# A two-layer decoder trunk: part of layer 1's down projection as seven block products

## The chip, the cores and the metric

The kernel runs on one core of a Trainium2 chip. The metric is the device time in microseconds of one execution; for each kernel the median of several runs is given.

## The reference

Input `x` is 1 x 512 x 1024 in float32. Two layers follow one another, each a mixer and a gated FFN with a convolution, both with a pre-RMSNorm and a residual, and a final RMSNorm. The part that matters here is the FFN (`D_FF` = 2816):

```python
def gated_conv_ffn(x, w_gate, w_up, conv_w, conv_b, w_down):
    g = jnp.einsum('bsd,df->bsf', x, w_gate)
    g = causal_dwconv3(g, conv_w) + conv_b
    up = jnp.einsum('bsd,df->bsf', x, w_up)
    return jnp.einsum('bsf,fd->bsd', jax.nn.silu(g) * up, w_down)
...
        hn = rms_norm(h, norm_ffn[layer])
        h = h + gated_conv_ffn(hn, w_ffn_gate[layer], w_ffn_up[layer], ...)
    return rms_norm(h, final_norm)
```

## The kernel before

The 2816 hidden channels are 22 tiles of 128 (`ft` = 0 to 21), the 512 tokens four tiles, the 1024 output columns two halves of 512. Every float32 factor is split in a high part (rounded to the fast float32r form, by ScalarE) and a low part (the rest, by VectorE), and each product is three matmuls: high x high, high x low, low x high (`mm3`, lines 132 to 135). `parts` (line 125) splits a weight tile of 128 x 1024 so. `summed` (line 116) does it without VectorE: ScalarE writes the negated high part, a DMA from GpSimd's queue adds the raw tile to it, and ScalarE writes the high part.

Hidden tiles are made in pairs `f`, `f` + 1. Pairs 0 and 2 are computed directly (`direct`). Pairs 4, 6, 10, 14, 18 go through `both`: the gate and the up projection are each cut into 2 x 2 blocks and computed with seven block products in place of eight (Strassen's way, in Winograd's form), from sums of weight blocks (`s12`, `s34`) and sums of activation blocks that stand ready (`t23`, `t41`). Pairs 8, 12, 16, 20 go through `seven`, which does so for the up projection alone; the gate is done directly (`gates(0)`, `gates(1)`). A `seven` or `both` product is 12 matmuls of 256 columns.

In layer 1 (`ffn1`) the down projection is done in groups, `PARTS`: after pairs 0 and 2 for tiles 0 and 1, after pair 4 for tiles 2 to 5, and from then on after every `both` and `seven` for four tiles. `act` (line 516) splits each activation tile into `a_hi` and `a_lo` as soon as it is there. `group8` (line 1035) multiplies: the stationary operand is an activation tile of 128 tokens, the moving one a weight row block of 512 columns; eight outputs (four token tiles, two halves) have a PSUM bank each, and when an output's last matmul is done VectorE adds the bank to `y` (line 1010). The last group also does the final norm and stores.

The order on each engine is not the program's. A scheduler takes what is ready by its own estimate, in order of place in the program, and gives out buffers in the same way; `inorder` (`keep_in_program_order`) pins an instruction behind the one traced before it on its engine. What limits how far it reaches ahead are the rings of buffers: `raw` 4 (weights as loaded), `whi` and `wlo` 6 each (split weights), `sum` 3 (sums of weights), `ahi` and `alo` 4 each (split activations), `s` 3, and seven PSUM banks.

Of the kernel before, what the change touches and what calls it, by code (L numbers as in the profile page):

```python
# [15 lines left out]
P = 128  # L16
# [14 lines left out]
def tile_trunk(ctx: ExitStack, tc: tile.TileContext, x, norm_mix, norm_ffn, final_norm,  # L31
# [99 lines left out]

    def mm3(ps, lhs, rhs, start, stop):
        nc.tensor.matmul(ps, lhs[0], rhs[0], start=start, stop=False)  # L133
        nc.tensor.matmul(ps, lhs[0], rhs[1], start=False, stop=False)  # L134
        nc.tensor.matmul(ps, lhs[1], rhs[0], start=False, stop=stop)  # L135
# [352 lines left out]
    class Ffn:  # L488
# [7 lines left out]

        def __init__(self, layer, prm, norm, ap, sums):
            self.layer, self.prm, self.ap, self.acts = layer, prm, ap, {}
            self.norm, self.sums = norm, sums
            self.t23, self.t41 = {}, {}  # L500

        def conv(self, t, ft):
            ap, prm, n = self.ap, self.prm, f"{self.layer}_{ft}"
            c = ap.tile([P, S], F32, tag="c", bufs=2, name=f"c{n}")
            nc.scalar.activation(c, t[:, 0:S], AF.Copy, scale=prm("cf", ft))
            for i in (1, 2):
                nc.vector.scalar_tensor_tensor(c, t[:, i : S + i], prm("cf", i * NF + ft), c,  # L507
                                               op0=ALU.mult, op1=ALU.add)
            return c

        def silu(self, c, ft):
            s = self.ap.tile([P, S], F32, tag="s", bufs=3, name=f"s{self.layer}_{ft}")
            nc.scalar.activation(s, c, AF.Silu, bias=self.prm("bf", ft))  # L513
            return s

        def act(self, ft, s):
            self.acts[ft] = split(self.ap, s, f"a{self.layer}_{ft}", tag="a", bufs=4)

# [190 lines left out]

        def seven(self, f):  # L710
            layer, ap, n = self.layer, self.ap, f"{self.layer}_{f}"
# [56 lines left out]
            def add(i, ps):  # L768
                nc.vector.tensor_tensor(kept[:, i, :], ps, kept[:, i, :], ALU.add)

            keep(0, multiply(1))
# [21 lines left out]
            nc.vector.tensor_tensor(s0, kept[:, :2, :], s0, ALU.mult)  # L793
            self.act(f, s[0])

        def hidden(self, f, before=lambda i, j: None):
            if f == 0:
                def first(i, j):
                    before(i, j)
                    if (i, j) == (1, 0):  # L800
                        self.norm.rstd_tokens()
                    elif (i, j) == (2, 2):
                        self.r = self.norm.rstd_spread()

                ch = self.pair_weights(0, [("g", 0), ("u", 0), ("g", 1), ("u", 1)])
                rest = self.direct(0, False, (range(4),), ch, first)
                self.ch = self.pair_weights(2, [("g", 0), ("g", 1), ("u", 0), ("u", 1)], "g")
                for kp in range(NP):
                    self.normalize(kp)
                rest()  # L810
            elif f == 2:
                self.direct(2, True, ((0, 1), (2, 3)), self.ch)()
            elif f % 4 == 2 or f == 4:
                self.both(f)
            else:
                self.seven(f)

# [142 lines left out]
    def ffn1(norm):  # L960
        with tc.tile_pool(name="f1", bufs=1) as ap:
# [3 lines left out]

            ffn = Ffn(1, prm1, norm, ap, sums)
            acts = ffn.acts
            y = [ap.tile([P, D], F32, name=f"y{t}") for t in range(NT)]
            ssf = ap.tile([P, NT, PAD], F32, name="ssf")[:, :, :2]
# [11 lines left out]

            for groups, a, b in PARTS:
# [24 lines left out]
                def done(j, ps):  # L1007
# [7 lines left out]
                    nc.scalar.activation(sq, dst, AF.Square, accum_out=ss)  # L1015
                    yf[half] = ap.tile([P, S], F32, tag="s", bufs=3, name=f"yf{j}")
                    nc.vector.tensor_tensor(yf[half], dst, fin[:, half * 512 : (half + 1) * 512],
# [17 lines left out]
    def group8(name, ks, lhs, rhs, tail, on_done):  # L1035
# [45 lines left out]
```

## Time and profile before

| | |
|---|---|
| median of 3 runs | 1005.43 us (1005.26 to 1005.86) |
| span of the profiled execution, first to last instruction | 1004.4 us |
| median less span | 1.0 us |
| TensorE busy | 992.1 us |
| VectorE busy | 666.0 us |
| ScalarE busy | 499.9 us |
| GpSimd busy | 94.1 us |
| mean granted TensorE clock | 0.999 |

Busy times are of the one profiled execution. PE is TensorE's matmuls, PEld its weight loads, DVE is VectorE, ACT ScalarE, POOL GpSimd, SP the queue that issues most loads. `u_8a` is the bank of product "a" of the up projection of pair 8, `dn` a bank of the down projection. A matmul's printed duration is its latency; start-to-start distances tell what one costs. In brackets behind a row stands the idle time ahead of it and what ended it.

### The profile page before, as it was taken

The numbers are of one execution on the slowest core, as the hardware profiler recorded it, in microseconds if no ns is written. First come the engines' busy times: TensorE is split into PE (matmuls) and PEld (weight loads), VectorE is DVE, ScalarE is ACT, GpSimd is POOL, SyncE is SP. The second block draws the span as 40 slices with busy tenths as digits, with TensorE's granted clock in tenths as the row PEclk, the third lists the DMA queues.
The fourth block names the chain that finished last, engine by engine and source line by source line (L and its number), as shares of the span: only waits on it lengthen the run. The fifth ranks groups of instructions, "written<-read, shape, count | busy, mean of one in ns | idle before, by whom it ended". The sixth has DMA issues, their size and how long they took to land.

```text
span 1004.4 us, 14019 instructions
## 1 busy us (share of the span) xinstructions
PE 992.1 (99%) x5547; PEld 865.9 (86%) x5547; DVE 666.0 (66%) x993; ACT 499.9 (50%) x735; POOL 94.1 (9%) x109
## 2 busy tenths in 40 slices
PE   8999999999999999999999999999999999999997
PEld 6888888898989989899878888888989898898985
DVE  5977457968584775847833645389675857658567
ACT  6523345754553635537645434675535365353553
POOL 3032030200000000000300001212000000000000
PEclk9999999999999999999999999999999999999999
DMA  7532234554445444454433123435545345353432
GB/s 236 178 105 84 85 90 122 117 155 114 118 142 131 128 110 119 138 137 127 127 125 104 63 85 105 101 88 123 150 100 153 105 127 147 94 152 112 127 85 84
DMA packets 80749, 120.30 MB, mean 120 GB/s; under 512 B 4164, under 2 KB 53548, under 8 KB 80684
## 3 DMA queue, kind: packets, MB, share of 16 engines
q1 hardware_dynamic: 73580, 98.96, 30.9%
q0 software_dynamic: 5760, 18.88, 10.7%
q10 hardware_dynamic: 1344, 1.58, 0.5%
q8 instruction: 43, 0.70, 0.3%
q14 instruction: 22, 0.18, 0.1%
HBM read 98.42 MB, written 2.10 MB: 100 GB/s over the span
## 4 chain that ended last, share of the span: by engine, by line
PE 95%; DMA 2%; DVE 2%; ACT 1%; SPq 0%; issue 0%; POOL 0%; DVEq 0%; ACTq 0%; POOLq 0%
PE dn L133 4%; PE dn L135 4%; PE dn L134 4%; PE d L133 4%; PE d L134 4%; PE d L135 4%; PE gu L133 3%; PE g L133 3%; PE g L134 3%; PE gu L134 3%; PE gu L135 3%; PE g L135 3%; PE u L135 1%; PE oo L133 1%; PE oo L135 1%; PE u L134 1%
## 5 line engine op out<-in xcount | busy, mean ns | idle before, releaser
L507 DVE SCALAR_TENSOR_TENSOR c<-rows,prm,c 128x512 f32<-128x512 f32 x88 | 68.9, 792 | 0.3
L134 PE MATMUL d<-a_lo,whi_d 128*128 128x512 f32 x176 | 68.6, 390 | 0.0
L135 PE MATMUL d<-a_hi,wlo_d 128*128 128x512 f32 x176 | 68.5, 389 | 0.0
L133 PE MATMUL dn<-whi_dn,a_hi 128*128 128x512 f32 x176 | 68.4, 390 | 0.0
L134 PE MATMUL dn<-wlo_dn,a_hi 128*128 128x512 f32 x176 | 68.4, 390 | 0.0
L135 PE MATMUL dn<-whi_dn,a_lo 128*128 128x512 f32 x176 | 67.6, 390 | 0.0
L133 PE MATMUL d<-a_hi,whi_d 128*128 128x512 f32 x176 | 67.1, 390 | 0.0
L1010 DVE TENSOR_TENSOR y<-dn,y 128x512 f32<-128x512 f32 x48 | 32.3, 688 | 30.9 <-PE dn L135 30.7
L133 PE MATMUL g<-hgh,whi_g 128*128 128x512 f32 x128 | 50.0, 391 | 0.0
L134 PE MATMUL g<-hgl,whi_g 128*128 128x512 f32 x128 | 50.0, 391 | 0.0
L135 PE MATMUL g<-hgh,wlo_g 128*128 128x512 f32 x128 | 49.8, 389 | 0.0
L129 DVE TENSOR_TENSOR wlo_dn<-raw_dn,whi_dn 128x1024 fp32r<-128x1024 f32 x22 | 26.8, 1222 | 30.7 <-ACT whi_dn L128 30.7
L129 DVE TENSOR_TENSOR wlo_d<-raw_d,whi_d 128x1024 fp32r<-128x1024 f32 x22 | 26.8, 1221 | 30.2 <-ACT whi_d L128 30.2
L129 DVE TENSOR_TENSOR wlo_u<-raw_u,whi_u 128x1024 fp32r<-128x1024 f32 x16 | 19.6, 1223 | 34.2 <-ACT whi_u L128 34.1
L120 ACT ACTIVATE wlo_g<-raw_g 128x1024 fp32r<-128x1024 f32 x14 | 14.7, 1050 | 51.6 <-PE dn L134 51.6
L292 DVE TENSOR_TENSOR h<-d,h 128x512 f32<-128x512 f32 x48 | 32.4, 686 | 11.6 <-PE d L135 11.1
L513 ACT ACTIVATE s<-c,prm 128x512 f32<-128x512 f32 x44 | 31.6, 718 | 16.7 <-DVE c L507 16.6
L135 PEld LDWEIGHTS dn<-whi_dn,a_lo 128*128 128x128 f32 x176 | 33.0, 188 | 7.4 <-DVE a_lo L249 0.2
L134 PEld LDWEIGHTS d<-a_lo,whi_d 128*128 128x128 f32 x176 | 33.1, 188 | 7.1 <-DVE a_lo L249 0.2
L133 PEld LDWEIGHTS dn<-whi_dn,a_hi 128*128 128x128 f32 x176 | 33.1, 188 | 7.0 <-ACT a_hi L247 0.2
L133 PEld LDWEIGHTS d<-a_hi,whi_d 128*128 128x128 f32 x176 | 32.9, 188 | 7.0
L135 PEld LDWEIGHTS d<-a_hi,wlo_d 128*128 128x128 f32 x176 | 33.0, 188 | 6.8
(972 smaller groups left out, 3196.0 us busy)
## 6 DMA issues: line engine op xcount, KB each, us to landing
raw_g<-in_w_ffn_gate_dram SPq DMA_DIRECT2D x36, 512.0 KB, 4.5
raw_u<-in_w_ffn_up_dram SPq DMA_DIRECT2D x36, 512.0 KB, 3.8
raw_d<-in_w_ffn_down_dram SPq DMA_DIRECT2D x22, 512.0 KB, 3.6
raw_dn<-in_w_ffn_down_dram SPq DMA_DIRECT2D x22, 512.0 KB, 4.4
wlo_u<-raw_u POOLq DMA_DIRECT2D x18, 512.0 KB, 5.2
wlo_g<-raw_g POOLq DMA_DIRECT2D x14, 512.0 KB, 4.5
raw_oe<-in_w_out_even_dram SPq DMA_DIRECT2D x8, 512.0 KB, 3.5
raw_g<-in_w_ffn_gate_dram SPq DMA_DIRECT2D x16, 256.0 KB, 2.9
```

What stands on the lines that cost most here:

```text
L120: nc.scalar.activation(lo, raw, AF.Copy, scale=-1.0)
L129: nc.vector.tensor_tensor(lo, raw, hi.bitcast(F32), ALU.subtract)
L133: nc.tensor.matmul(ps, lhs[0], rhs[0], start=start, stop=False)
L134: nc.tensor.matmul(ps, lhs[0], rhs[1], start=False, stop=False)
L135: nc.tensor.matmul(ps, lhs[1], rhs[0], start=False, stop=stop)
L292: nc.vector.tensor_tensor(h[k], ps, h[k], ALU.add)
L507: nc.vector.scalar_tensor_tensor(c, t[:, i : S + i], prm("cf", i * NF + ft), c, op0=ALU.mult, op1=ALU.add)
L513: nc.scalar.activation(s, c, AF.Silu, bias=self.prm("bf", ft))
L1010: nc.vector.tensor_tensor(dst, ps, dst, ALU.add)
```

## The change

Tiles 2 to 17 of layer 1's down projection leave `group8`. Four tiles `a` to `a` + 3 are taken as a 2 x 2 block product: two pairs of hidden tiles, two halves of the tokens, two halves of the columns. `down(a)` computes it with seven block products of 12 matmuls (128 x 512) instead of 96 matmuls in one go. It is a generator: each `yield` ends a step, and `seven` calls `step()` at eight places between its own products, so the down products of tiles 2 to 5 lie within pair 8, those of 6 to 9 within pair 12, 10 to 13 within 16, 14 to 17 within 20. Each product accumulates in a bank (`a`, `b` or `e`, one per token tile), and after each product VectorE adds its two banks to `y`. The sums of weights are t1 (in place, in the first raw tile) and t2, t3, t4 in tiles of their own (ring `sum`). The activations are kept unsplit, in pairs (ring `s`, now four tiles of 128 x 2 x 512), and split when a product needs them (`part`, ring `ahi`/`alo`, now three). The down projection of tiles 0 and 1 now follows pair 4 instead of pair 2. Tile 20 is split into a `sum` tile. `c` moves to another pool, `y` becomes one tile, and `group8` pins the first matmul of each three.

```diff
-    def mm3(ps, lhs, rhs, start, stop):
-        nc.tensor.matmul(ps, lhs[0], rhs[0], start=start, stop=False)
+    def mm3(ps, lhs, rhs, start, stop, order=lambda ins: ins):
+        order(nc.tensor.matmul(ps, lhs[0], rhs[0], start=start, stop=False))
...
-            c = ap.tile([P, S], F32, tag="c", bufs=2, name=f"c{n}")
+            c = tp.tile([P, S], F32, tag="sq", name=f"c{n}")
...
         def silu(self, c, ft):
-            s = self.ap.tile([P, S], F32, tag="s", bufs=3, name=f"s{self.layer}_{ft}")
+            f = ft - ft % 2
+            if f not in self.rows:
+                self.rows[f] = self.ap.tile([P, 2, S], F32, tag="s",
+                                            bufs=4 if self.layer else 3,
+                                            name=f"s{self.layer}_{f}")
+            s = self.rows[f][:, ft % 2, :]
             nc.scalar.activation(s, c, AF.Silu, bias=self.prm("bf", ft))
             return s
 
         def act(self, ft, s):
-            self.acts[ft] = split(self.ap, s, f"a{self.layer}_{ft}", tag="a", bufs=4)
+            if ft == NF - 2 and self.kept:
+                both = self.ap.tile([P, 2, S], F32R, tag="sum", bufs=3, name="a_last")
...
+            elif ft not in self.kept:
+                self.acts[ft] = split(self.ap, s, f"a{self.layer}_{ft}", tag="a",
+                                      bufs=4 if self.layer == 0 else 3)
...
             keep(0, multiply(1))
+            step()
             gates(0)
+            step()
             keep(1, multiply(6))
             gates(1)
+            step()
             c, s = [], []
             for j in range(2):
                 t = padded_tile()
                 nc.scalar.copy(t[:, 2:], banks[j])
                 c.append(self.conv(t, f + j))
+            step()
             keep(2, multiply(7))
             for j in range(2):
                 s.append(self.silu(c[j], f + j))
+            step()
             ps = multiply(5)
+            step()
             p2 = multiply(2)
             add(2, ps)
             add(0, p2)
+            step()
             ps = multiply(4)
...
             self.act(f, s[0])
+            step()
...
+            def part(a, src, n):
+                hi = ap.tile([P, 2, HALF], F32R, tag="ahi", bufs=3, name=f"hi{n}_{a}")
+                lo = ap.tile([P, 2, HALF], F32R, tag="alo", bufs=3, name=f"lo{n}_{a}")
+                nc.scalar.activation(hi, src, AF.Copy)
+                nc.vector.tensor_tensor(lo, src, hi.bitcast(F32), ALU.subtract)
+                return hi, lo
+
+            def down(a):
...
+                g1, g2 = ffn.rows[a], ffn.rows[a + 2]
+                a11, a21 = g1[:, :, :HALF], g1[:, :, HALF:]
+                a12, a22 = g2[:, :, :HALF], g2[:, :, HALF:]
...
+                def multiply(product, at, half, c):
+                    (hi, lo), (whi, wlo) = stat[product], mov[product]
+                    for i in range(2):
+                        first = (at, i) not in banks
+                        if first:
+                            banks[at, i] = mm_bank(f"{name}{at}{i}")
+                        ps = banks[at, i]
+                        ts_ = slice(i * P, (i + 1) * P)
+                        for k in range(2):
+                            for l, r, end in ((hi, whi, False), (hi, wlo, False),
+                                              (lo, whi, k == 1)):
+                                nc.tensor.matmul(ps, l[:, k, ts_], r[:, k, :], start=first,
+                                                 stop=end, skip_group_check=True)
+                                first = False
+                        dst = y[2 * half + i][:, c * 512 : (c + 1) * 512]
+                        nc.vector.tensor_tensor(dst, ps, dst, ALU.add)
...
+                b11, b12, b22, b21 = block(0, 0), block(0, 1), block(1, 1), block(1, 0)
+                mov[1] = parts(*b11)
+                stat[1] = part(a, a11, 1)
+                t1 = b11[0]
+                minus(t1, b12[0], b11[0])
...
+                nc.vector.tensor_tensor(s1, a21, a22, ALU.add)
+                minus(s2, s1, a11)
+                yield
+                multiply(1, "a", 0, 0)
+                stat[2] = part(a, a12, 2)
+                mov[2] = parts(*b21)
+                t2 = t_tile(2)
+                minus(t2, b22[0], t1)
+                yield
+                multiply(2, "b", 0, 0)
+                stat[6] = part(a, s2, 6)
+                mov[6] = parts(t2, 2, 512, f"{name}_t2")
+                yield
+                multiply(6, "a", 0, 1)
+                stat[5] = part(a, s1, 5)
+                mov[5] = parts(t1, 2, 512, f"{name}_t1")
+                t3 = t_tile(3)
+                minus(t3, b22[0], b12[0])
+                minus(s1, a11, a21)
+                yield
+                multiply(5, "e", 1, 1)
+                stat[7] = part(a, s1, 7)
+                mov[7] = summed(t3, 2, 512, f"{name}_t3")
+                minus(s2, a12, s2)
+                yield
+                multiply(7, "a", 1, 1)
+                stat[3] = part(a, s2, 3)
+                mov[3] = parts(*b22)
+                t4 = t_tile(4)
+                minus(t4, b21[0], t2)
+                yield
+                multiply(3, "e", 0, 1)
+                stat[4] = part(a, a22, 4)
+                mov[4] = summed(t4, 2, 512, f"{name}_t4")
+                yield
+                multiply(4, "a", 1, 0)
+                yield
+
+            for groups, a, b in (((0, 2, 4), 0, 2), ((6, 8), 2, 6), ((10, 12), 6, 10),
+                                 ((14, 16), 10, 14), ((18, 20), 14, 18), ((), 18, 22)):
                 for f in groups:
-                    ffn.hidden(f, before=before)
+                    steps = down(a) if f > 6 and f % 4 == 0 else None
+                    ffn.hidden(f, before=before, steps=steps)
                 last = b == NF
+                if a in (2, 6, 10, 14):
+                    continue
...
-            mm3(banks[j], lhs(ks[i], j), rhs(ks[i], j), i == 0, i == len(ks) - 1)
+            mm3(banks[j], lhs(ks[i], j), rhs(ks[i], j), i == 0, i == len(ks) - 1, inorder)
```

More of the change, by code (lines that the diff above doesn't have):

```diff
@@ L488, in tile_trunk, with __init__ @@
     class Ffn:
-        def __init__(self, layer, prm, norm, ap, sums):
+        def __init__(self, layer, prm, norm, ap, sums, kept=()):
             self.layer, self.prm, self.ap, self.acts = layer, prm, ap, {}
@@ L708, in both, with seven @@
             self.act(f, s[0])
-        def seven(self, f):
+        def seven(self, f, steps=None):
             layer, ap, n = self.layer, self.ap, f"{self.layer}_{f}"
@@ L769, in add, with step @@
                 nc.vector.tensor_tensor(kept[:, i, :], ps, kept[:, i, :], ALU.add)
+            def step():
+                if steps is not None:
+                    next(steps)
             keep(0, multiply(1))
+            step()
             gates(0)
+            step()
             keep(1, multiply(6))
             gates(1)
+            step()
             c, s = [], []
@@ L794, in seven, with hidden @@
             self.act(f, s[0])
-        def hidden(self, f, before=lambda i, j: None):
+            step()
+        def hidden(self, f, before=lambda i, j: None, steps=None):
             if f == 0:
@@ L815, in hidden @@
             else:
-                self.seven(f)
+                self.seven(f, steps)
     def ffn0(norm):
@@ L964, in sums @@
                         for k in (kp, kp + NP)]
-            ffn = Ffn(1, prm1, norm, ap, sums)
+            ffn = Ffn(1, prm1, norm, ap, sums, range(2, 18))
             acts = ffn.acts
-            y = [ap.tile([P, D], F32, name=f"y{t}") for t in range(NT)]
+            y_all = ap.tile([P, NT, D], F32, name="y")
+            y = [y_all[:, t, :] for t in range(NT)]
             ssf = ap.tile([P, NT, PAD], F32, name="ssf")[:, :, :2]
@@ L980, in before, with minus @@
                     turn_residual(j, i)
-            for groups, a, b in PARTS:
+            def minus(dst, x, y_):
+                nc.vector.tensor_tensor(dst, x, y_, ALU.subtract)
+            def part(a, src, n):
[4 more added lines that the diff above has]
+                return hi, lo
@@ L1015, in done @@
                     nc.scalar.activation(sq, dst, AF.Square, accum_out=ss)
-                    yf[half] = ap.tile([P, S], F32, tag="s", bufs=3, name=f"yf{j}")
+                    if half == 0:
+                        yf["pair"] = ap.tile([P, 2, S], F32, tag="s", bufs=4, name=f"yf{j}")
+                    yf[half] = yf["pair"][:, half, :]
                     nc.vector.tensor_tensor(yf[half], dst, fin[:, half * 512 : (half + 1) * 512],
```

19 lines of the change are left out of this document (17 added, 2 removed).

## The prediction

> **What bounds the kernel now.** I read the page first (busy shares, then the chain that ended last), then the windows of one period of layer 1's FFN, then the PE, VectorE and ScalarE timelines inside it, and last the waits.
>
> ```profile
> span 1004.4 us, 14019 instructions
> PE 992.1 (99%) x5547; PEld 865.9 (86%) x5547; DVE 666.0 (66%) x993; ACT 499.9 (50%) x735; POOL 94.1 (9%) x109
> ...
> PE 95%; DMA 2%; DVE 2%; ACT 1%; SPq 0%; issue 0%; POOL 0%; DVEq 0%; ACTq 0%; POOLq 0%
> ```
>
> TensorE is busy 99% of the span and holds 95% of the chain: time goes only by taking matmuls away or by making them wait. The profiled span is 1004.4 us and the median of the runs is 1005.43, so 1.0 us lies outside the span; I work out the change of the span and add it to the median. Layer 1's FFN repeats a period: a pair of hidden tiles by `both`, a pair by `seven`, then the down projection of four tiles. The windows of one period, in that order (columns: us, PE, PEld, DVE, ACT, POOL busy with counts, clock, DMA share, GB/s), and then the whole period:
>
> ```profile
> 745.80:764.70 18.90, 18.90 (x159) 18.79 (x158) 12.08 (x18) 10.95 (x18) 0.86 (x1) 1.00 0.57 157
> 764.70:785.70 21.00, 21.00 (x134) 19.09 (x133) 14.52 (x22) 13.86 (x22) 0.85 (x1) 1.00 0.55 151
> 785.70:809.00 23.30, 23.30 (x111) 19.48 (x110) 15.53 (x25) 6.03 (x7) 0.86 (x1) 1.00 0.28 77
> ```
> ```profile
> 745.80:809.00 63.20, 63.20 (x399) 57.35 (x398) 42.13 (x63) 30.85 (x46) 2.57 (x3) 1.00 0.46 125
> ```
>
> TensorE has no gap, at full clock. VectorE has 21 us of 63.2 to spare, ScalarE 32.
>
> **What goes.** The first matmul of this period's down projection, and the first behind it:
>
> ```profile
> 785.55 0.40 PE L133 MATMUL dn<-whi_dn,a_hi 128*128 128x512 f32 x1
> ...
> 807.36 0.28 PE L624 MATMUL g_10a<-hgh,whi_a 128*128 128x256 f32 x1
> ```
>
> In between are 4 tiles x 8 outputs x 3 = 96 matmuls in 21.81 us: 0.227 us each (the 0.40 printed is latency; they are pipelined). Seven products of 2 x 2 x 3 = 12 matmuls of the same shape make 84, so a group saves 12 x 0.227 = 2.73 us. Four groups are changed (tiles 2-5, 6-9, 10-13, 14-17): 10.9 us. A kernel that stays dense on TensorE would take 1005.4 - 10.9 = 994.5 us; that is the floor.
>
> **What comes on VectorE.** The groups of the next period, and four rows of the VectorE timeline for the true spacing:
>
> ```profile
> L1010 DVE TENSOR_TENSOR y<-dn,y 128x512 f32<-128x512 f32 x8 | 5.4, 690 | 7.7 <-PE dn L135 7.7
> L129 DVE TENSOR_TENSOR wlo_dn<-raw_dn,whi_dn 128x1024 fp32r<-128x1024 f32 x4 | 4.9, 1221 | 6.4 <-ACT whi_dn L128 6.4
> L249 DVE TENSOR_TENSOR a_lo<-s,a_hi 128x512 fp32r<-128x512 f32 x4 | 2.7, 684 | 0.0
> ```
> ```profile
> 746.30 1.22 DVE L634 TENSOR_TENSOR wlo_s12u<-s12u,whi_s12u 128x1024 fp32r<-128x1024 f32 x1
> 747.43 0.69 DVE L730 TENSOR_TENSOR s<-raw_u,raw_u 128x512 f32<-128x512 f32 x1
> 748.03 0.69 DVE L732 TENSOR_TENSOR s<-raw_u 128x512 f32<-128x512 f32 x1
> 748.64 0.69 DVE L731 TENSOR_TENSOR s<-s,raw_u 128x512 f32<-128x512 f32 x1
> ```
>
> Back to back, a 1024-wide instruction takes 1.13 us from start to start and a 512-wide one 0.605. Before, a group has 4 wide (`wlo_dn`) and 12 narrow (4 `a_lo`, 8 additions to `y`): 4 x 1.13 + 12 x 0.605 = 11.8 us. After, it has 9 wide (t1 to t4, five `parts`) and 25 narrow (four sums of activations, seven low parts, 14 additions): 10.2 + 15.1 = 25.3 us. That is 13.5 us more. The period becomes 63.2 - 2.7 = 60.5 us for TensorE and 42.1 + 13.5 = 55.6 us for VectorE, 92% of it. The stretch in which the products lie, `seven` and down together, is 21.0 + 23.3 - 2.7 = 41.6 us for TensorE, and holds 14.5 + 15.5 + 13.5 = 43.5 us for VectorE: 1.9 us too much, which must go into `both`'s stretch, where 18.9 - 12.1 = 6.8 us are idle. What can go there is the work that is already split over that border, sums and low parts for the next `both`; its later products need it 6 to 13 us after the border.
>
> [...] By whole durations the sum would be a rival of its own (the third below).
>
> **What comes on ScalarE, GpSimd and the queues.**
>
> ```profile
> L128 ACT ACTIVATE whi_dn<-raw_dn 128x1024 fp32r<-128x1024 f32 x22 | 23.2, 1055 | 18.2 <-PE g L134 14.0 <-issue 1.6 <-PE u_4a L624 1.5
> L247 ACT ACTIVATE a_hi<-s 128x512 fp32r<-128x512 f32 x44 | 27.5, 627 | 21.3 <-DVE s L793 9.0 <-DVE s L707 6.4 <-DVE s L789 4.0
> L120 ACT ACTIVATE wlo_u<-raw_u 128x1024 fp32r<-128x1024 f32 x18 | 18.8, 1045 | 0.0
> L122 ACT ACTIVATE whi_u<-raw_u 128x1024 fp32r<-128x1024 f32 x18 | 18.9, 1048 | 1.2 <-PE d L134 1.2
> ```
>
> Before: 4 x 1.06 + 4 x 0.63 = 6.7 us. After: five `parts` 5.3, two `summed` with two passes each 4.2, seven high parts 4.4: 13.9 us. ScalarE goes from 30.9 to 38.1 us of 60.5; its cover is 22 us of idle time, so as a sum it costs nothing. SP issues four 512 KB loads for a group as before. GpSimd's queue gets two accumulating copies more:
>
> ```profile
> L121 POOL DMA_DIRECT2D wlo_u<-raw_u x18: 852/862/867, 206.9 to 959.2; - x18
> ...
> DMA to landing us min/median/max: 4.5/5.2/7.6
> ```
>
> One such pair needs 1.05 (negated copy) + 0.86 (issue) + 5.2 (landing) = 7.1 us. Its weight tiles come free when product 2 ends (before that, `seven`'s own six units fill the six buffers), and product 7 needs them after products 6 and 5 (2.73 us each) and `seven`'s products 7 and 5. Those take 1.44 us each:
>
> ```profile
> 764.72 1.44 PE u_8a L624 x12
> ```
>
> That is 8.3 us of cover for 7.1: 1.2 us to spare with the median landing, nothing with the 7.6 one. The other copy (product 4) has some 14 us.
>
> **Handoffs.** The waits before show what the buffers do (columns: total us, times, longest):
>
> ```profile
> ACT whi_dn L128 <- PE g L134: 14.0, 4, 3.5
> ```
> ```profile
> SPq L110 <- DVE wlo_dn L129: 40.0, 12, 6.7
> ```
>
> The second group of down weights already waits until `gates(1)` lets go of a gate weight tile. After, product 6's weights take that tile. They need 1.06 + 1.22 = 2.3 us, and the rest of `gates(1)` (6 matmuls, 1.4 us) and product 2 (2.7 us) cover it. The activations of a product come from tiles that are done a period earlier, so unlike now no product waits for a fresh `silu`. The four raw tiles are held longer (t1 is built in the first, the fourth is needed until t4), so the next `both`'s loads come later, but loads for it still land before its first product. Accumulating a second product into a bank waits for the addition that reads it; the closest pair is products 1, 6 and 7 with 5 us and more between them, more than VectorE's queue should lag. I charge one late handoff per group: a ScalarE pass and a low part, 2.3 us, behind a cover of one `seven` product, 1.44 us, so 0.9 us; bounds 0 and 2.3. Four groups: 3.4 us, bounds 0 and 9.
>
> **Two edges.** First: tiles 4 and 5 now come before the down projection of tiles 0 and 1, so `both`'s first products no longer have that projection ahead of them.
>
> ```profile
> 667.00:703.00 36.00, 36.00 (x164) 29.93 (x163) 36.00 (x56) 25.18 (x38) 7.72 (x7) 1.00 0.44 100
> ```
> ```profile
> 691.37 0.39 PE L133 MATMUL dn<-whi_dn,a_hi 128*128 128x512 f32 x1
> ```
> ```profile
> 704.35 1.22 DVE L634 TENSOR_TENSOR wlo_s12u<-s12u,whi_s12u 128x1024 fp32r<-128x1024 f32 x1
> ```
>
> VectorE is busy all of these 36 us. The fifth product of `both` needs that `wlo_s12u`; it would be due at 691.4 + 4 x 1.44 = 697.2. Ahead of the row, 8 additions, 2 `wlo_dn` and 2 `a_lo` move behind or vanish: 4.8 + 2.3 + 1.2 = 8.3 us, so it ends at 704.4 + 1.2 - 8.3 = 697.3. No margin, no debt: 0, bounds -0.5 and 3. Second: in the last group activations 18 and 19 keep two of three `a` buffers, so products 2, 6, 5, 7, 3 take the third in turn. Each handoff is 0.63 + 0.68 = 1.3 us, with a `seven` product of 1.44 us to put in between. I take 0.3 us for the lot; with one wide VectorE instruction (1.13) in front of each of four it would be 4. `c` in another pool and `s` in pairs change no operation.
>
> Sum: 994.5 + 3.4 + 0.3 = 998.2; I say 998.
>
> **The rivals.** (1) VectorE sets the pace of the mixed stretch, slower than before. Its queue is in order, and additions that wait for TensorE stand in front of the operands of the next product:
>
> ```profile
> 802.12 0.69 DVE L1010 TENSOR_TENSOR y<-dn,y 128x512 f32<-128x512 f32 x1 [2.03 <-PE dn L135]
> ```
>
> The stretch took 44.3 us, and VectorE's work in it is 43.5. If nothing can be put off into `both`'s stretch, it loses as soon as VectorE idles over 0.8 us in it. With two additions that each wait for half a product (6 x 0.227 = 1.36 us) it is 46.2 us, 1.9 more than now, 7.7 in four groups: 1013 us. For it: 92% occupancy, and 7.7 us of such waits per period now. Against: those waits fell where VectorE had nothing else, and 6.8 us of slack stand next door. (2) The accumulating copy for product 7 lands late: 7.6 instead of 5.2, and 1 us of queueing on ScalarE, is 2.2 us late per group; with everything else as forecast 998.2 + 4 x 2.2 = 1007, and half of that if another product is put in front: 1003. (3) VectorE's instructions don't overlap: 81 per period by 0.085 us is 6.9 us, so up to 62.5 us per period, which is 0.7 less than now: 1005.4 - 2.8 = 1002.6. The spacing rows say no. [...] (4) The change doesn't do what it says: the products bunch up behind `seven` instead of lying between, since the scheduler places them by what is ready; then six of the seven are dense and the handoffs lose their covers, 1.4 us each: 4 x 6 x 1.4 = 34 us lost, 1028.
>
> **How the numbers follow.** Forecast 0.60 (its own range 994.5 to 1002); (1) 0.24, (2) 0.10, (3) 0.02, (4) 0.04. 0.2% is 2 us, about what a measurement of this kernel can tell from no change. Faster (below 1003.4): the forecast less 0.03 for its upper bounds, the near half of (2), and (3): 0.57 + 0.05 + 0.02 = 0.64. Same: that 0.03 and the far half of (2), 1007: 0.08. Slower: (1) and (4): 0.28. The range 994 to 1013 leaves out (4) and the upper half of (1), and a little below.
>
> **What would show it.** Right: 48 matmuls fewer; a period of 60.5 to 62 us with TensorE over 97% busy and VectorE at some 56 us; the ends of `both` and the down products with no wait over 1 us. Wrong: VectorE without idle time through the mixed stretch while TensorE waits on low parts or on additions (rival 1), TensorE waiting on product 7 for the copy (rival 2), a VectorE sum over 60 us (rival 3), or `dn` matmuls in a block (rival 4).

## The result, and the profile after

The changed kernel takes 996.3 us in the median of 4 runs (995.47 to 996.59), the kernel before 1005.35 us beside it (1004.01 to 1005.86): a ratio of 0.991, interval 0.9896 to 0.9924. That is 9.0 us faster; 7.4 had been forecast.

The head of the page of the changed kernel, and the shares of its chain:

```profile
span 993.7 us, 14101 instructions
PE 982.4 (99%) x5499; PEld 857.3 (86%) x5499; DVE 719.3 (72%) x1065; ACT 527.9 (53%) x767; POOL 100.8 (10%) x117
...
PE 93%; issue 3%; DVE 2%; ACT 1%; DMA 0%; POOL 0%; DVEq 0%; ACTq 0%; POOLq 0%
```

The matmuls are 48 fewer, as they should be (5547 before). VectorE has 53.3 us more, in four groups 13.3 each, and TensorE is still busy 99% of the time. The period has its own windows: the whole one that begins with pair 10, then its two parts, `both` and the mixed stretch (`seven` and the down products). The columns are us, PE, PEld, DVE, ACT and POOL busy with counts, clock, DMA share, GB/s.

```profile
782.06:842.30 60.24, 60.24 (x387) 54.96 (x386) 55.33 (x81) 37.82 (x54) 4.29 (x5) 1.00 0.56 149
```
```profile
782.06:802.20 20.14, 20.14 (x171) 20.14 (x170) 17.56 (x27) 11.85 (x19) 0.85 (x1) 1.00 0.55 158
802.20:842.30 40.10, 40.10 (x219) 34.82 (x218) 37.77 (x55) 25.97 (x36) 3.44 (x4) 1.00 0.57 144
```

TensorE has no gap in this period and runs at full clock. From the first matmul of one `both` to the first of the next it takes 60.28 us (781.90 to 842.18), where it took 63.17 (807.36 to 870.53). VectorE's 55.3 us divide into 17.6 of 20.1 and 37.8 of 40.1. These windows begin about one product, 1.44 us, earlier in the period than those of the prediction; when the profile before is cut at the first matmul of each part too, VectorE has 13.3 us in `both`'s stretch and 28.8 in the mixed one.

All waits of TensorE that the view lists in layer 1's FFN (columns: total us, times, longest):

```profile
PE u_4e L638 <- DVE wlo_s12u L648: 0.6, 1, 0.6
PE dn14e L1042 <- ACT hi L1015: 0.3, 1, 0.3
PE u_4a L638 <- ACT kept L696: 0.3, 1, 0.3
```

None lies in the three full periods. The copy for product 7 is the closest thing to one. Its issue, the first matmul that reads it, and the landing times of the two down copies in this stretch, first the one issued at 763.0 us (product 7), then the one issued at 768.8 (product 4):

```profile
763.01 0.86 POOL L121 DMA_DIRECT2D wlo_dn_t<-t  x1 [15.67 <-ACT wlo_dn_t L120]
```
```profile
769.59 0.40 PE L1042 MATMUL dn2a<-wlo_dn_t,hi 128*128 128x512 f32 x1
```
```profile
DMA to landing us min/median/max: 5.2/5.2/5.2
```
```profile
DMA to landing us min/median/max: 6.4/6.4/6.4
```

The copy for product 7 is issued 6.6 us ahead of its use and lands after 5.2, at 768.2: 1.4 us to spare. In the three later groups it lands after 5.1, 5.1 and 4.6 us, and the copy for product 4, which has more time, after 6.3, 6.3 and 6.7.

Not all of the difference of the two spans (1004.4 and 993.7) is the change's. Ahead of layer 1's FFN stands a GpSimd instruction that is the same in both kernels, and its duration varies from profile to profile. From the kernel before, from the changed kernel, and from the second profile of the same changed kernel (`a0_after` below):

```profile
L844 POOL TENSOR_SCALAR_AFFINE_SELECT ws<-ws x1: 2010/2010/2010, 505.4 to 505.4; 128x1024 f32<-128x1024 f32 x1
```
```profile
L870 POOL TENSOR_SCALAR_AFFINE_SELECT ws<-ws x1: 1092/1092/1092, 504.2 to 504.2; 128x1024 f32<-128x1024 f32 x1
```
```profile
L870 POOL TENSOR_SCALAR_AFFINE_SELECT ws<-ws x1: 1772/1772/1772, 505.8 to 505.8; 128x1024 f32<-128x1024 f32 x1
```

The second profile of the changed kernel has a span of 996.2 us, 2.5 more than the first, and is already 2.3 us behind it (713.0 against 710.7 us) at the first down matmul of layer 1. TensorE's wait for this instruction, 1.6 us before and absent in the first profile of the changed kernel, is back in the second with 1.5 us, so it is not the change's. So single spans can tell no more than about 2 us here; periods can be read much finer. From the start of the edge around pair 4 to the last matmul of the program it is 305.3 us before (691.4 to 996.7), and 296.8 (689.2 to 986.0) and 297.0 (691.4 to 988.4) in the two profiles of the changed kernel: 8.3 to 8.5 us less, gained in the part that was changed.

### The profile page after: what moved, and what is told of

It is laid out like the page before. It is cut to its first block, busy times and chain, and to the rows that moved or that the text cites. A ratio compares the mean times of both kernels' runs of the same rounds, so it can differ in the third digit from the quotient of the medians.

```text
span 993.7 us, 14101 instructions
## 1 busy us (share of the span) xinstructions
PE 982.4 (99%) x5499; PEld 857.3 (86%) x5499; DVE 719.3 (72%) x1065; ACT 527.9 (53%) x767; POOL 100.8 (10%) x117
## 4 chain that ended last, share of the span: by engine, by line
PE 93%; issue 3%; DVE 2%; ACT 1%; DMA 0%; POOL 0%; DVEq 0%; ACTq 0%; POOLq 0%
PE d L133 4%; PE d L135 4%; PE d L134 4%; PE g L133 3%; PE g L134 3%; PE g L135 3%; PE gu L133 2%; PE gu L135 2%; PE gu L134 2%; PE v L133 1%; PE oo L135 1%; PE u L133 1%; PE u L134 1%; PE oo L134 1%; PE u L135 1%
## 5 line engine op out<-in xcount | busy, mean ns | idle before, releaser
L121 POOL DMA_DIRECT2D wlo_u<-raw_u x18 | 15.4, 858 | 265.3 <-ACT wlo_u L120 182.9
L129 DVE TENSOR_TENSOR wlo_g<-raw_g,whi_g 128x1024 fp32r<-128x1024 f32 x20 | 24.4, 1219 | 14.0 <-ACT whi_g L128 14.0
L189 POOL TENSOR_TENSOR ssq_f<-ssq_f,sq_f 128x512 f32<-128x512 f32 x12 | 16.3, 1358 | 179.8 <-ACT sq_f L188 144.9
L175 ACT ACTIVATE hgh<-h,prm 128x512 fp32r<-128x512 f32 x24 | 17.3, 720 | 32.0 <-DVE h L292 32.0
L176 DVE SCALAR_TENSOR_TENSOR hgl<-h,prm,hgh 128x512 fp32r<-128x512 f32 x24 | 22.1, 922 | 15.0 <-ACT hgh L175 14.9
L128 ACT ACTIVATE whi_d<-raw_d 128x1024 fp32r<-128x1024 f32 x22 | 23.2, 1055 | 17.7 <-PE g L134 14.0
L506 ACT ACTIVATE c<-rows,prm 128x512 f32<-128x512 f32 x44 | 31.6, 719 | 1.6 <-DVE rows L701 1.0
L128 ACT ACTIVATE whi_g<-raw_g 128x1024 fp32r<-128x1024 f32 x20 | 21.0, 1051 | 19.9 <-PE u_18a L638 4.2
```

The lines of the kernel that those rows point to most:

```text
L128: nc.scalar.activation(hi, raw, AF.Copy)
L129: nc.vector.tensor_tensor(lo, raw, hi.bitcast(F32), ALU.subtract)
L175: nc.scalar.activation(hg[k][0], h[k], AF.Copy, scale=g)
L176: nc.vector.scalar_tensor_tensor(hg[k][1], h[k], g, hg[k][0].bitcast(F32), op0=ALU.mult, op1=ALU.subtract)
L189: nc.gpsimd.tensor_tensor(self.ssq, self.ssq, sq, ALU.add)
```

## The experiments

### The two edges, and the changed kernel again

`a0_after` is the changed kernel, unedited. `e2_order_back` computes the down projection of tiles 0 and 1 ahead of pair 4 again. `e3_late_split` splits the activations 18 and 19 late, so that they hold no `a` buffers, and takes the last tiles in the order 18, 20, 21, 19. `e4_both_edges` is both.

```diff
-            for groups, a, b in (((0, 2, 4), 0, 2), ((6, 8), 2, 6), ...
+            for groups, a, b in (((0, 2), 0, 2), ((4, 6, 8), 2, 6), ...      # e2, e4
...
-            ffn = Ffn(1, prm1, norm, ap, sums, range(2, 18))
+            ffn = Ffn(1, prm1, norm, ap, sums, range(2, 20))                 # e3, e4
...
+                    for ft in (18, 19):                                      # e3, e4
+                        acts[ft] = split(ap, ffn.rows[18][:, ft - 18, :], f"a1_{ft}", tag="a",
+                                         bufs=3)
```

> The changed kernel itself, timed beside the variants of this series. Theory (TensorE is the bound, 48 matmuls of 0.227 us are gone, all but the two edges is covered): 996 to 997 us, and the wait ahead of the transposes of w_spatial (1.6 us in the profile of before, none in that of the change) comes and goes with the execution. Rival (part of the gain lies in layer 0 and the mixer, from the other pool for c and the pairs of s): that wait is absent here again and present in every profile of before.

> One part undone: the down projection of tiles 0 and 1 goes back ahead of pair 4. Theory: the 1.4 us that both(4) lost on its fifth product (the low part of s12u came 0.6 us late, the bank 0.3 us later) go away, since the projection gives VectorE 10.9 us: 1.4 us less than the changed kernel, 995. Rival (VectorE's backlog is only put off, and the y additions fall into both(4)): no difference, within 0.5 us.

> One change at the last group: activations 18 and 19 stay unsplit in their pair tile and are split after the last down products, so that these have all three a buffers; the last projection takes its tiles in the order 18, 20, 21, 19. Theory: the 1.3 us that the last mixed stretch is longer than the others go away: 995. Rival (that time is from the loads of the last weights or from VectorE, whose load there is 39.4 of 41.4 us): no difference, or up to 1 us more for the later splits.

> Both of the edits before together. Theory: the two edges add up, 2.7 us less than the changed kernel, 993.6 us, which is the floor of 48 matmuls. Rival: the sum is smaller than 1 us.

Measured, in the same order: 997.39 us (996.73 to 998.07), 996.26 (996.21 to 996.96), 996.97 (996.4 to 997.77), 996.11 (995.64 to 997.29). The ratios to the kernel before overlap: 0.9922 (0.9907 to 0.9936), 0.991 (0.9894 to 0.9927), 0.9918 (0.9903 to 0.9933), 0.9911 (0.9896 to 0.9925). The traces tell more than these times, and less than was expected. From the start of this edge to the first product of pair 6, `a0_after` takes 32.5 us (691.4 to 723.9) and `e2_order_back` 32.2 (690.9 to 723.1): 0.3 us, not 1.4. The wait that was to go is still there in `e2_order_back`, on the same low part:

```profile
PE u_4e L638 <- DVE wlo_s12u L648: 0.9, 1, 0.9
```

At the other edge, from the first product of pair 20 to the last matmul, `e3_late_split` takes 63.1 us (925.2 to 988.3) and `a0_after` 63.3 (925.1 to 988.4), since the late split is waited for in turn in the last projection:

```profile
PE dn L135 <- DVE a_lo L249: 1.1, 1, 1.1
```

The mixed stretch of pair 20 alone is back to 40.13 us in `e3_late_split`, as in a full period; it took 41.5 in the first profile of the changed kernel. The late splits free the `a` buffers and also take VectorE's work out of that stretch (36.4 us where it had 39.5), and which of the two did it was not separated; the last projection loses 1.1 us again. `a0_after` took 0.4 us more than expected, and the expectations for the three variants failed: at the first edge the same low part is late in either order, and at the other the lateness moves on to the last projection. No version is shown to beat the changed kernel.

### The products in a row

`e1_bunched` hands out all steps of `down` but the first, which prepares product 1, at one place, behind product 2 of `seven`, in place of spreading them.

```diff
             def step():
-                if steps is not None:
-                    next(steps)
+                pass
 
             keep(0, multiply(1))
-            step()
+            if steps is not None:
+                next(steps)
...
             add(0, p2)
-            step()
+            if steps is not None:
+                for _ in steps:
+                    pass
```

> The seven down products are issued in a row, behind product 2 of seven, in place of between its products; their count and operands are the same. Theory (placement is what covers the handoffs): each product must have its operands within 2.7 us of the one before, and VectorE's additions and low parts fall together; some 2 us are lost in each of four groups, 1004 us (bounds 998 and 1012). Rival (TensorE's count alone matters, six weight buffers and three a buffers carry it): 996 to 997 as with the changed kernel.

Measured 999.28 us (998.48 to 1000.12), ratio 0.9943 (0.9927 to 0.996): some 2 to 3 us slower than the changed kernel. In the trace the full periods lose nothing. Its windows of the same two parts:

```profile
784.10:804.30 20.20, 20.20 (x170) 20.20 (x170) 18.22 (x29) 12.84 (x20) 0.85 (x1) 1.00 0.64 176
804.30:844.30 40.00, 40.00 (x218) 34.78 (x218) 36.36 (x53) 24.32 (x34) 3.44 (x4) 1.00 0.53 133
```

60.2 us again, without a gap, though the expectation had 2 us lost in each of four groups. What is lost is lost from pair 20 on: it begins at 924.6 us, against 925.1 in `a0_after`, and from there to the last matmul it is 65.6 us, against 63.3. The fourth rival had priced six handoffs of 1.4 us per group; in the full periods none was paid. It took the operands of a product as made between two products. They aren't: a product's preparation stands one step ahead of it, and the scheduler gives it to VectorE and ScalarE while products further up run.

### More work for VectorE

`e5_dve4` and `e6_dve8` repeat the subtraction that makes t3 four and eight times more, in place, so that VectorE has 4.5 and 9.0 us more per group.

```diff
-                minus(t3, b22[0], b12[0])
+                for _ in range(5):          # e6_dve8: range(9)
+                    minus(t3, b22[0], b12[0])
```

> The subtraction that makes t3 is done four times more per group with the same result: 4 x 1.13 = 4.5 us more on VectorE in each period, which then holds 59.8 us of 60.3. Theory (5 us of slack that can be used): 0 to 2 us lost per group, 997 to 1004 us. Rival (VectorE already sets the pace of the mixed stretch): the full 4.5 us in each of four groups, 1014 us.

> The same subtraction eight times more: 9 us more per period, VectorE 64.4 us against TensorE's 60.3. Theory: VectorE now is the bound, the period grows by 4.1 us and what cannot be moved, 4 to 7 us in each of four groups: 1013 to 1024 us. Rival (VectorE set the pace before): 9 us each, 1032 us. If VectorE's extra work were hidden anyway: 997.

Measured 1035.03 us (1034.46 to 1037.68), ratio 1.0305 (1.029 to 1.0321), and 1055.33 (1053.95 to 1056.56), ratio 1.0502 (1.0486 to 1.0517). Against 997.4 that is 9.4 and 14.5 us per group, more than the work itself and more than either theory or rival had. In `e5_dve4` the first stalls of a period are for product 7 (PE timeline; in brackets the idle time ahead of the row and what ended it):

```profile
773.18 0.73 PE L1042 MATMUL dn2a<-whi_dn_t,hi 128*128 128x512 f32 x2 [0.84 <-ACT whi_dn_t L122]
...
778.41 0.70 PE L1042 MATMUL dn2a<-wlo_dn_t,hi 128*128 128x512 f32 x1 [2.36 <-DMA wlo_dn_t<-t]
```

The copy behind t3 is late now. Its chain had 1.4 us to spare, and the repeated subtractions stand at its head. What the stall leaves behind, in windows right after it:

```profile
775.00:778.40 3.40, 1.05 (x7) 0.76 (x6) 2.03 (x4) 2.71 (x4) 0.85 (x1) 1.00 1.01 182
778.40:781.40 3.00, 2.99 (x7) 2.39 (x8) 0.55 (x1) 0.00 (x0) 0.00 (x0) 0.52 0.92 241
781.40:784.40 3.00, 3.00 (x13) 2.43 (x12) 2.28 (x5) 0.63 (x1) 0.00 (x0) 0.91 0.96 204
```

The granted clock is 0.52 for 3 us and 0.91 for the next 3: 1.7 us lost behind a stall of 2.4. In `e6_dve8` the longest wait of a group, 4.4 to 4.6 us, is another one, in the mixed stretch itself: a product of `seven` waits until VectorE has added the one ahead of it in its bank to `kept`. No run comes nearer to the first rival.

```profile
PE u_8e L638 <- DVE kept L783: 4.4, 1, 4.4
```

At this point two explanations stood: A, the chain with the copy; B, VectorE's load as such. These two kernels change both at once.

### Less work for TensorE

`e7_two_matmuls` leaves the product of low activation and high weight out of the seven products, 28 of 84 matmuls per group; the output is less exact by that.

```diff
-                            for l, r, end in ((hi, whi, False), (hi, wlo, False),
-                                              (lo, whi, k == 1)):
+                            for l, r, end in ((hi, whi, False), (hi, wlo, k == 1)):
```

> Leaves out the matmul of low activations by high weights in the seven products (28 of 84 per group): the down projection of tiles 2 to 17 loses that correction. TensorE needs 28 x 0.227 = 6.4 us less per group, 53.9 us per period, VectorE 55.3 as before. Theory: the gain follows TensorE until VectorE's 55.3 us per period bind: 3 to 5 us less in each of four groups, 977 to 985 us. Rival 1 (VectorE sets the pace now): no gain, 996. If only matmuls counted: 971.

Measured 1015.15 us (1015.08 to 1016.9), ratio 1.0107 (1.0091 to 1.0122). TensorE has 25 us less to do and the kernel is 18 us slower. No expectation came near that. The parts of one period, and TensorE's four longest waits in it:

```profile
781.80:808.10 26.30, 22.37 (x171) 21.02 (x170) 20.54 (x30) 14.43 (x21) 1.71 (x2) 0.98 0.60 161
808.10:851.00 42.90, 36.65 (x190) 30.33 (x190) 34.69 (x51) 22.98 (x33) 2.58 (x3) 0.96 0.45 111
```
```profile
PE dn6a L1041 <- DMA wlo_dn_t<-t: 5.0, 2, 4.1
PE g_10b L638 <- DMA wlo_g<-raw_g: 1.5, 1, 1.5
PE g_10e L638 <- ACT whi_s12g L647: 1.4, 1, 1.4
PE dn6a L1041 <- DVE wlo_dn L129: 1.1, 1, 1.1
```

Here shorter products cover less of the copies, and the weight sums of the next `both` (`whi_s12g`, `wlo_g`) are late too. Again both A and B fit.

### Load without a chain, and chains without copies

`e10_spare14` adds 14 subtractions per group in a tile of their own, which nothing waits for. `e12_no_copy` replaces the two accumulating copies by VectorE subtractions, and `e11_two_no_copy` does so in `e7_two_matmuls`.

```diff
+            spare = ap.tile([P, 256], F32, name="spare")                  # e10
+            nc.vector.memset(spare, 0.0)
...
+                    for _ in range(2):                                    # e10, ahead of
+                        minus(spare, spare, spare)                        # each of seven yields
...
-                mov[7] = summed(t3, 2, 512, f"{name}_t3")
+                mov[7] = parts(t3, 2, 512, f"{name}_t3")                  # e11, e12
...
-                mov[4] = summed(t4, 2, 512, f"{name}_t4")
+                mov[4] = parts(t4, 2, 512, f"{name}_t4")                  # e11, e12
```

> Fourteen subtractions of 128x256 numbers in a tile of their own are added to each group, two behind each of the first seven preparations: 14 x 0.335 = 4.7 us of VectorE per group, as much as the four repeated subtractions of the earlier experiment (4.5 us), but in no chain that a product waits for. Theory A (what made that experiment slow was the chain subtraction, ScalarE, accumulating copy, matmul): 997 to 1001 us, no wait of TensorE for wlo_dn_t over 1 us. Theory B (VectorE's load as such: 60.0 of 60.3 us busy): about 1035 us, as in that experiment, the same waits.

> As the kernel with two of three matmuls per block (the low activation with the high weight is left out of the seven products), and the low parts of the weight sums of products 7 and 4 are made by a VectorE subtraction instead of an accumulating copy: two copies fewer and 2 x 1.13 us of VectorE more per group. Theory A (the copies were what came late when TensorE had less to do): TensorE 54 us and VectorE about 57.5 us per group, so the time falls to 985 to 990 us. Theory B (VectorE's load): 1015 us or more, since VectorE has more to do than in the kernel that took 1015 us.

> The changed kernel, with the low parts for products 7 and 4 made by VectorE subtractions instead of accumulating copies (2.3 us of VectorE more per group, 57.6 of 60.3 us; 8 copies of 512 KB fewer). Theory A (chain, not load): 996 to 998 us, as the changed kernel, since its copies are not late. Theory B (load): half of what 4.5 us did, 1007 to 1016 us.

Measured: `e10_spare14` 998.18 us (997.75 to 998.55), ratio 0.9928 (0.9911 to 0.9945); `e11_two_no_copy` 1011.01 (1009.58 to 1012.58), ratio 1.0055 (1.004 to 1.007); `e12_no_copy` 1013.0 (1011.19 to 1014.57), ratio 1.0074 (1.0059 to 1.0089).

`e10_spare14` lies where theory A put it, but it does not refute B as far as it was meant to. Its subtractions depend on nothing, so the scheduler drew most of them forward into idle time of earlier stretches; the last starts at 800.5 us. Only eight of the 56 are left behind the start of pair 8. The windows below are those of the changed kernel, and this kernel begins pair 8 1.5 us and pair 10 2.3 us later. Cut at its own first matmuls, the mixed stretch of pair 8 (743.24 to 784.18 us) holds six of them, 39.7 us of VectorE, and is 0.8 us longer than in the changed kernel; in the next period two are left, VectorE has 57.2 us, and TensorE loses nothing.

```profile
741.94:782.06 40.12, 39.65 (x220) 34.31 (x219) 38.92 (x59) 25.23 (x35) 3.42 (x4) 1.00 0.52 129
782.06:842.30 60.24, 60.24 (x385) 54.96 (x385) 57.19 (x85) 37.90 (x54) 4.29 (x5) 1.00 0.60 154
```

`e12_no_copy` refutes A. No down product has a copy to wait for, and yet some 16 us are lost. (`e11_two_no_copy` lies between what A and B had said and decides nothing.) The time is in theory B's range, but B does not say where it is lost. The two parts of a period do:

```profile
783.80:808.40 24.60, 22.13 (x171) 21.78 (x170) 20.05 (x30) 13.75 (x21) 1.70 (x2) 0.93 0.59 161
808.40:848.50 40.10, 40.10 (x218) 34.82 (x218) 37.65 (x54) 21.78 (x32) 0.85 (x1) 1.00 0.35 99
```

The mixed stretch is as it was: 40.1 us, 37.7 us of VectorE. The 2.3 us of added work don't fit in it and reappear in `both`'s stretch (20.05 in place of 17.56 us), and that stretch is 4.4 us longer. What comes late there: first the weight sum, in the changed kernel and in this one (their `both` begins at 781.90 and 783.65),

```profile
774.07 0.68 DVE L668 TENSOR_TENSOR s12g<-s12g,raw_g 128x512 f32<-128x512 f32 x1
```
```profile
780.00 0.68 DVE L668 TENSOR_TENSOR s12g<-s12g,raw_g 128x512 f32<-128x512 f32 x1
```

4.2 us later against its group. The next load of up weights waits until VectorE has read the gate's raw tile (`s34g`, right behind `s12g`), and is later by the same 4.2 us:

```profile
775.43 0.37 SPq L110 DMA_DIRECT2D raw_u<-in_w_ffn_up_dram  x1
```
```profile
781.36 0.37 SPq L110 DMA_DIRECT2D raw_u<-in_w_ffn_up_dram  x1
```

Then the issue of the copy for `wlo_u`, 3.3 us behind the start of `both` in the first and 7.7 in the second,

```profile
785.16 0.85 POOL L121 DMA_DIRECT2D wlo_u<-raw_u  x1 [6.70 <-PE u_10a L638]
```
```profile
791.38 0.85 POOL L121 DMA_DIRECT2D wlo_u<-raw_u  x1 [5.53 <-ACT wlo_u L120]
```

and last, in `e12_no_copy`, the product that reads it, with the clock around the stall:

```profile
798.23 0.39 PE L638 MATMUL u_10b<-hgh,wlo_u 128*128 128x256 f32 x1 [2.47 <-DMA wlo_u<-raw_u]
```
```profile
795.30:798.20 2.90, 0.46 (x4) 0.26 (x3) 2.90 (x5) 1.59 (x3) 0.00 (x0) 1.00 0.74 147
798.20:801.20 3.00, 2.97 (x16) 2.97 (x17) 2.44 (x6) 0.00 (x0) 0.00 (x0) 0.59 0.54 130
801.20:804.20 3.00, 3.00 (x23) 3.00 (x23) 1.80 (x4) 1.12 (x3) 0.00 (x0) 0.84 1.02 374
```

A stall of 2.5 us, then 3.0 x 0.41 + 3.0 x 0.16 = 1.7 us of lower clock: 4.2 of the 4.4. Three such stretches (pairs 10, 14, 18) make 13.2 us; most of the rest is a wait of 2.0 us for a `wlo_dn` in the final group, behind which matmuls start 0.43 us apart (984.34 to 986.47 us) where 0.23 is usual. So a third theory, C: VectorE is as good as full in the mixed stretch, at some 37.7 us of 40.1, and what doesn't fit is the next `both`'s weight sums, which are last in its queue; their lateness moves the copies, and past the copies' cover TensorE stops.

### The same chains, with VectorE's load as it was

`e14_no_copy_fewer_adds` is `e12_no_copy` without the additions of products 3 and 7 to `y`.

```diff
+                        if product in (3, 7):
+                            continue
                         dst = y[2 * half + i][:, c * 512 : (c + 1) * 512]
                         nc.vector.tensor_tensor(dst, ps, dst, ALU.add)
```

> As the kernel without the two accumulating copies, which took 1013.0 us, but the additions of products 3 and 7 to y are left out (four of 0.605 us per group: the output lacks them), so that VectorE has about as much to do per group as in the changed kernel: 55.3 + 2.3 - 2.4 = 55.2 us. Theory C (a queue of VectorE's work at the end of the mixed stretch, which makes the weight sums of the next group late, its copies and the release of its raw tiles with them): 996 to 999 us, no wait of TensorE over 1 us, the copy for wlo_u issued about 3 us behind the first matmul of that group, as in the changed kernel, and not 7.7 us. Theory D (the place of the two subtractions in the products' own chains, or the PE order planned around them, whatever VectorE's load): about 1013 us, with the same waits of 2.4 us for wlo_u.

Measured 996.38 us (995.53 to 996.91), ratio 0.9914 (0.9898 to 0.9931). The two parts of the period, and the copy for `wlo_u` (`both` begins at 783.03):

```profile
783.20:803.34 20.14, 20.14 (x170) 20.14 (x170) 17.27 (x26) 11.67 (x18) 0.85 (x1) 1.00 0.67 175
803.34:843.46 40.12, 40.12 (x219) 34.83 (x218) 37.75 (x53) 24.18 (x34) 1.71 (x2) 1.00 0.40 110
```
```profile
786.29 0.85 POOL L121 DMA_DIRECT2D wlo_u<-raw_u  x1 [4.65 <-DVE wlo_s12u L648]
```

VectorE is back at 17.3 and 37.75 us, the copy is issued 3.3 us behind the start of `both`, and the 16.6 us are gone. C holds, D falls in its first form: the subtractions in the products' chains cost nothing by themselves. One thing stays mixed up: in `e12_no_copy` the scheduler also cut three products of `both` (`g_10b`, `u_10e`, `u_10a`) into pieces and interleaved these, and here it did not. That order was not tried alone.

## Why the prediction was right

The floor. 12 matmuls of 0.227 us less per group: the full period went from 63.17 to 60.28 us, 2.89 where 2.73 was worked out; the rest lies in `both`, which took 20.33 us before, with 0.18 us lost at `g_10a`'s second product (812.3 us), and takes 20.15 now. The prediction's windows count one product of `both` with the down stretch; cut at the first matmuls, the mixed stretch was 42.84 us, and 42.84 - 2.73 is the 40.1 that was measured. The sum for VectorE, 55.6 us per period, was measured at 55.3, that for ScalarE, 38.1, at 37.8. So spacing from start to start was the right price, and the third rival falls with it: a sum by whole durations would have had 62.5 us in a period that took 60.28. The trace after has the same spacing: `s12g`, `s34g` and an addition to `y`, 512 wide and one behind the other (834.35, 834.95 and 835.55 us), start 0.60 us apart where 0.68 is printed.

The term that was too large: one late handoff per group, 0.9 us, 3.4 in all. It was 0 in the three full periods; TensorE waits for nothing there. The steps that prepare a product stand far enough ahead, which `e1_bunched` shows most plainly. The terms that were too small: the edges, 0.3 us in all. In the trace `both` of pair 4 takes 21.6 us where 14 products at 1.44 take 20.2, with the wait for `wlo_s12u` on which the prediction saw "no margin, no debt"; and the last stretch of pair 20 takes some 1.3 us more than a full period's. Both lie within the bounds given (3 and 4). 994.5 + 0 + 1.4 + 1.3 = 997.2, and the runs say 996.3 and 997.4. By this sum the change gains 8.2 us; by the traces 8.3 to 8.5. The two errors, 3.4 us too much and 2.4 too little, nearly cancelled, which was luck. `e2_order_back` and `e3_late_split` show that the edges aren't repaired by undoing the one choice that seemed to cause them.

What was right about the copy for product 7: 8.3 us of cover for 7.1. The tile came free at 761.0, the first matmul stands at 769.35: 8.3. The copy landed at 768.2, 7.2 us behind the first of these, and left 1.4 us to its first reader. The parts of the 7.1 were not quite right: the landing counts from the start of the issue (of the copies for `wlo_u`, one issued at 785.16 lands after 6.9 us and one at 806.77 after 4.5, and the loads that wait for them are issued at 792.15 and 811.37), so the 0.86 us of issue were counted twice; in their place ScalarE began 0.65 us after the tile was free, and GpSimd 0.3 us after ScalarE. `e5_dve4`, which puts 4.5 us into this chain, stalls right there. The second rival was thus close: the copy for product 4, later in the same stretch, took 1.2 us more to land, nearly all that product 7 had to spare.

The first rival was the real danger: VectorE's load has little room. But what the next 2.3 us ran into was not its mechanism. `e12_no_copy`, with 2.3 us of VectorE more per group, takes 1013 us, which was the rival's price too, but for the changed kernel and on another way, so that is a coincidence. TensorE does not lose in the mixed stretch there, through additions in front of operands; that stretch stays at 40.1 us. It loses one stretch later. Only with 9 us more, in `e6_dve8`, does TensorE wait long for VectorE's additions in the mixed stretch. The prediction had seen that work must be put off into `both`'s stretch (1.9 us by its sum; 17.6 - 13.3 = 4.3 in the trace, with 2.3 us of the mixed stretch idle) and had counted the 6.8 us of idle time there as room. Room isn't what decides: it is which instructions are put off, and when their reader comes. In the changed kernel the copy for `wlo_u` still comes in time; with the put-off work 2.5 us longer it is 4.4 us later and TensorE waits 2.5. So the copy had some 2 us to spare, and less than 2.3 us of VectorE per period use them up; that close the changed kernel is to losing what it gained.

The fourth rival's price, 34 us, was wrong by more than ten times: the bunched kernel is 2 to 3 us slower, lost behind the full periods.

What stays open: why `e7_two_matmuls`, with 25 us of matmuls less, is slower than the kernel before rather than merely not faster. TensorE sits idle for 41.2 us of its span, against 13.5 in `a0_after`. The stalls of the copies (5.0 us in the mixed stretch of pair 12), late sums and low clock behind some of the stalls (0.53 from 779 to 782 us) are in its trace, and taking the copies away (`e11_two_no_copy`) brings back only 4 of 18 us, with waits for `wlo_g` and `wlo_a` in their place; how they feed one another wasn't taken apart.

## What to carry to other kernels

When work is traded from the engine that sets the time to one that runs beside it, sum the second engine's work by stretch, not by span, and follow what falls over the edge of a full stretch to its reader: its due time is the margin, not the idle time next door. Take start-to-start distances for such sums; here they gave VectorE's within 1%. The same kernel with 2.3 us of VectorE more in a period of 60 was slower than before the change, so test the margin by adding work in the chain that others wait for, not by work that the scheduler can place freely.

## What the runs showed of the hardware

A stall can cost more than its length. Behind stalls of TensorE of 2.36 us (`e5_dve4`) and 2.47 us (`e12_no_copy`) the granted clock was 0.52 and 0.59 over the next 3 us and 0.91 and 0.84 over the 3 after, 1.7 us lost each time. The length alone doesn't decide it. Behind a stall of 1.20 us in `e5_dve4` (866.8 us) the clock was 0.57 and 0.86, 1.7 us again; behind this one of 2.83 us, also in `e5_dve4`, it stayed at 1.00:

```profile
919.95 0.50 PE L1042 MATMUL dn10a<-wlo_dn_t,hi 128*128 128x512 f32 x1 [2.83 <-DMA wlo_dn_t<-t]
```
```profile
919.95:922.95 3.00, 3.00 (x13) 2.51 (x14) 1.43 (x3) 0.00 (x0) 0.00 (x0) 1.00 1.01 250
```

Behind the waits of 0.64 and 0.26 us in `both` of pair 4 of the changed kernel (694.6 to 698.2 us) it stayed at 1.00:

```profile
694.60:698.20 3.60, 2.70 (x20) 2.30 (x20) 2.10 (x3) 3.60 (x6) 0.87 (x1) 1.00 0.50 152
698.20:701.20 3.00, 3.00 (x27) 3.00 (x26) 2.47 (x3) 1.96 (x3) 0.00 (x0) 1.00 0.87 165
```

So a clock of 0.52 to 0.59 over 3 us followed stalls of 1.20, 2.36 and 2.47 us here, and 1.00 followed the one of 2.83 us. What decides which of the two it is, no run here shows.

The landing of an accumulating copy of 512 KB took 5.2 and 6.4 us within one stretch, and in each of the four groups the second took longer than the first (4.6 to 5.2 and 6.3 to 6.7 us). One unchanged GpSimd instruction took 1.09 us in one profile and 1.77 in another of the same kernel.
